# A hybrid decoder step: fewer transposes and products for the prompt's compressed branch and for a masked key block

## The chip, the cores and the metric

The kernel runs on one core of a Trainium2 chip. The core has TensorE (PE in the profile, with its weight loads as PEld), VectorE (DVE), ScalarE (ACT), GpSimd (POOL) and SyncE (SP), which work side by side and wait for each other through semaphores; 16 DMA engines move data. The metric is the device time of one execution in microseconds, as the median of several runs.

## What is computed

One layer of a decoder trunk is run on a prompt of 512 tokens and on 8 samples of 4 tokens. One input projection feeds two groups of eight heads: native sparse attention (three branches: compressed blocks, selected blocks, sliding window) and forgetting attention. The outputs are gated, multiplied by one output projection, and normed. What matters here is cut from the reference:

```python
def nsa_block(q, q_pos, gates, kc, vc, c_end, ks, vs, kw, vw, w_pos, slopes):
    ...
    p_c = masked_softmax(s_c, dist_c >= 0)
    o_c = jnp.einsum('bhgtn,bnhd->bthgd', p_c.astype(vc.dtype), vc)
    ...
    o = g[..., 0:1] * o_c + g[..., 1:2] * o_s + g[..., 2:3] * o_w

def fox_block(q, q_pos, dq, k, v, dk, k_pos):
    ...
    p = masked_softmax(s, k_pos[None, :] <= q_pos[:, None])
    return jnp.einsum('bhts,bshd->bthd', p.astype(v.dtype), v)
```

The prompt has 512 / 32 = 16 compressed keys, so `p_c` of a block of 128 queries is 128 x 16 for each head. In `fox_block` a query block sees no key block behind it.

## The kernel before

**Precision.** [...] `mm3` (L394) issues three products: hi x hi, hi x lo and lo x hi.

**What fills the time.** `run_tiles` (L515) computes the input projection: 60 tiles of 128 columns, each with 4 pieces of weights (`raw`, loaded from `w_in`, split into `whi` and `wlo`), into the PSUM tile `pz`, 272 tokens at a time. Its products are called pz products below. A piece is used by 24 of them, 12 for each half of the tokens; its split is issued two pieces ahead of use, and its load four splits ahead. `run_outputs` (L589) computes the output projection at the end, into `po`.

**What sets the order.** All other work (compression, both groups of heads on prompt and samples) is written as Python generators, the side streams. After every three pz products, `pump` (L223) lets each stream that is ready go on to its next `yield`. What is ready is decided by a clock that the recording layer keeps with its own costs for every instruction (class `Clock`); nothing of it is left at run time. The result is one fixed order for each engine. So a stream that issues less, or waits elsewhere, moves everything recorded after it. Every instruction goes through one helper line (L169), which is why the profile shows that line alone; groups are told apart by the names of their tiles.

**Forgetting attention on the prompt** (`fox_prompt`, L897). For each of 8 heads and each of two pairs of query blocks (`pr`), scores go to `fp` (probabilities, one tile for each of the two query blocks, `il`). The stream `apply` (L906) turns them: for each pair of key blocks (`jc`), four transposes of 128 x 128 into one PSUM tile `tr` (L923 to L927), then the split into `fpth` and `fptl` (128 x 512 each), then products with the split values `fvh`, `fvl` into `accf`. In the last pair of key blocks, the second one is masked for the first query block; those columns are filled with zeros (L987) and turned like the rest.

**Sparse attention on the prompt** (`nsa_prompt`, L1360). For each of two K/V heads, two pairs of query heads and four query blocks (16 jobs), the probabilities of the selected and the window branch are in tiles `np`, those of the compressed branch in `npc` (128 x 2 x 17; the last column is padding). The stream `apply` (L1378) turns `np` block by block, splits it into `npth` and `nptl` and multiplies by the values `nv0`, `nv1` into `acc`. At last it turns `npc`, one transpose of 128 x 16 for each of the two heads (L1413), splits the 16 x 256 result into `nptch` and `nptcl`, and adds three products with the compressed values `vcph`, `vcpl` (L1429). These tiles have 128 rows, of which 16 are filled and 112 hold zeros. `vcz` (L1386) is the load of the 16 rows of values.

**Samples.** `nsa_sample` (L1534) follows `nsa_prompt`; after it a tile `mx` is made, and `mix` (L1828) multiplies each head's output by its gate path, from loads. The output projection needs these heads one after another.

## Time and profile before

| what | us |
|---|---|
| median of 3 runs | 1379.68 |
| lowest, highest | 1375.85, 1386.52 |
| profiled execution, its own time | 1380.05 |
| span of the profiled execution | 1378.4 |

The page of the profile gives the busy time of each engine, the granted clock of TensorE in 40 slices (9 is 90% or more), and a chain of waits followed back from the last instruction. The view by windows gives busy times by stretch of the span, in us from its start; the timeline gives single instructions. The touched jobs run from 470 us (first transposes of `npc`) to 859 us (last), and from 518 us to 1073 us (first transposes of `fp` to last products into `accf`); the output products start at 1170 us.

### The profile page before, as it was taken

Reading aid. Unit: us, or ns where it says so; the run is one execution under the profiler, and the core shown is the slowest. Engines: PE = TensorE matmul, PEld = TensorE weight load, DVE = VectorE, ACT = ScalarE, POOL = GpSimd, SP = SyncE. Lnnn points to the kernel's source line nnn. Section 1 sums busy time; section 2 is a strip of 40 time slices with the busy share of each in tenths; the row PEclk is TensorE's granted clock in tenths of the full one; section 3 lists DMA queues with packets and bytes.
Section 4 is the critical chain, followed back from the end, with each engine's and each line's share of the span. In section 5 each row is a group of like instructions: output and inputs, shape, how many; then the busy total and the mean of one; then the engine's idle time right before and its main releaser. Section 6 shows DMA issues by size and latency. Waiting matters only on the chain.

```text
span 1378.4 us, 27307 instructions
## 1 busy us (share of the span) xinstructions
PE 1309.4 (95%) x10149; PEld 1151.8 (84%) x10149; DVE 789.9 (57%) x1982; ACT 544.6 (40%) x1167; POOL 276.2 (20%) x357
## 2 busy tenths in 40 slices
PE   8999898889999999998999999999999999999997
PEld 6899777778879999997888888788788899777786
DVE  6737655667644576655457774366466445444346
ACT  5224222323333467751224454136655423333222
POOL 3402435453430000004243302211110200000000
PEclk8999999999999999999999999999999999999999
DMA  6566667676998454467765758998788695234423
GB/s 193 170 168 192 204 176 224 206 231 196 282 298 243 116 145 150 147 180 219 254 201 178 217 151 247 249 255 218 222 207 187 209 321 162 72 121 147 129 90 130
DMA packets 303664, 265.65 MB, mean 193 GB/s; under 512 B 83058, under 2 KB 250850, under 8 KB 302860
## 3 DMA queue, kind: packets, MB, share of 16 engines
q1 hardware_dynamic: 279372, 187.30, 47.8%
q0 software_dynamic: 24016, 76.10, 17.4%
q8 instruction: 79, 1.29, 0.4%
q10 hardware_dynamic: 144, 0.52, 0.1%
q14 instruction: 53, 0.43, 0.1%
HBM read 235.68 MB, written 36.49 MB: 197 GB/s over the span
## 4 chain that ended last, share of the span: by engine, by line
PE 85%; DMA 5%; DVE 3%; issue 3%; ACT 1%; another core or an unknown queue 1%; SPq 1%; DVEq 0%; ACTq 0%
PE pz L169 48%; PE po L169 14%; PE s L169 6%; PE accv L169 5%; PE tr L169 5%; PE acc L169 3%; PE psb L169 2%; PE accf L169 1%; SPq L169 1%; DMA spg<-in_state_nsa_win 1%; DMA xt<-in_x_prompt 1%; DMA fpg<-in_cache_fox_kv 1%; DMA raw<-in_w_in 1%; PE pre L169 1%
## 5 line engine op out<-in xcount | busy, mean ns | idle before, releaser
L169 PE MATMUL pz<-h_hi,whi 128*128 128x272 f32 x1920 | 568.1, 296 | 11.2 <-ACT zt L169 4.7
L169 PE MATMUL pz<-h_hi,wlo 128*128 128x272 f32 x1920 | 557.6, 290 | 4.3 <-issue 3.5
L169 PE MATMUL pz<-h_lo,whi 128*128 128x272 f32 x1920 | 557.3, 290 | 3.7 <-issue 3.7
L169 PEld LDWEIGHTS pz<-h_hi,whi 128*128 128x128 f32 x1920 | 366.2, 191 | 30.1 <-issue 19.6
L169 PEld LDWEIGHTS pz<-h_lo,whi 128*128 128x128 f32 x1920 | 365.8, 191 | 5.4 <-issue 4.8
L169 PEld LDWEIGHTS pz<-h_hi,wlo 128*128 128x128 f32 x1920 | 365.3, 190 | 4.9 <-issue 3.8
L169 ACT ACTIVATE whi<-raw 128x512 fp32r<-128x512 f32 x275 | 171.6, 626 | 276.0 <-PE pz L169 142.8
L169 DVE TENSOR_TENSOR wlo<-raw,whi 128x512 fp32r<-128x512 f32 x275 | 185.9, 676 | 143.9 <-ACT whi L169 131.8
L169 POOL DMA_INDIRECT fpg<-in_cache_fox_kv,fi x128 | 127.6, 997 | 352.3 <-DMA raw<-in_w_in 205.9
L169 DVE TENSOR_TENSOR zt<-pz,rsb 128x272 f32<-128x272 f32 x61 | 26.9, 441 | 131.9 <-PE pz L169 128.1
L169 PE MATMUL po<-whi,h_hi 128*128 128x512 f32 (+1 forms) x256 | 95.5, 373 | 0.0
L169 PE MATMUL po<-whi,h_lo 128*128 128x512 f32 (+1 forms) x256 | 93.4, 365 | 0.0
L169 PE MATMUL po<-wlo,h_hi 128*128 128x512 f32 (+1 forms) x256 | 93.4, 365 | 0.0
L169 POOL DMA_INDIRECT crow<-in_cache_nsa_kv,ci x64 | 64.4, 1007 | 123.1 <-DVE ct L169 85.9
L169 ACT ACTIVATE zt<-pz 128x272 f32<-128x272 f32 x60 | 23.8, 396 | 155.0 <-PE pz L169 110.2
L169 DVE STREAM_TRANSPOSE ft<-fpg 128x1024 f32<-128x1024 f32 x64 | 78.6, 1232 | 8.9 <-PE accv L169 2.9
L169 POOL DMA_DIRECT2D spg<-in_cache_nsa_kv x64 | 35.0, 547 | 183.7 <-DVE skt L169 60.2
L169 PE MATMUL accv<-ft,fqb 128*32 128x256 f32 x512 | 51.0, 402 | 21.1 <-issue 19.8
L169 ACT ACTIVATE cxh<-ct 128x580 fp32r<-128x580 f32 (+1 forms) x64 | 42.2, 659 | 70.7 <-DVE ct L169 46.6
L169 DVE TENSOR_TENSOR cxl<-ct,cxh 128x580 fp32r<-128x580 f32 (+1 forms) x64 | 45.9, 717 | 39.2 <-ACT cxh L169 35.4
L169 PEld LDWEIGHTS po<-whi,h_hi 128*128 128x128 f32 x256 | 48.1, 188 | 19.7 <-ACT whi L169 7.5
L169 POOL DMA_DIRECT2D fpg<-in_cache_fox_kv x64 | 34.9, 545 | 135.6 <-PE accv L169 65.7
(412 smaller groups left out, 1965.8 us busy)
## 6 DMA issues: line engine op xcount, KB each, us to landing
raw<-in_w_in SPq DMA_DIRECT2D x240, 256.0 KB
fpg<-in_cache_fox_kv POOLq DMA_DIRECT2D x64, 256.0 KB
fpg<-in_cache_fox_kv SPq DMA_DIRECT2D x64, 256.0 KB
raw<-in_w_out SPq DMA_DIRECT2D x40, 256.0 KB
spg<-in_cache_nsa_kv POOLq DMA_DIRECT2D x64, 128.0 KB
spg<-in_cache_nsa_kv SPq DMA_DIRECT2D x64, 128.0 KB
out<-in_state_nsa_win SPq DMA_DIRECT2D x32, 254.0 KB
scr_z<-zt SPq DMA_DIRECT2D x28, 272.0 KB
```

The costliest lines, as they stand in the source:

```text
L169: return fn(*a, **k)
```

## The change

Three things are written otherwise.

*Forgetting attention.* In the last pair of key blocks the transpose of the masked block is left out. The two key blocks change places in the PSUM tile (`1 - jl`), so that the three turned blocks lie side by side; 384 columns are split instead of 512, and the first 128 columns of `fpth` and `fptl` are set to zero by VectorE. The memset of the masked columns of `fp` goes.

*Compressed probabilities.* The split is made before the transpose. A new tile `npx` (two of them, used in turn) holds for each of two heads 64 columns: the 16 rounded probabilities, the 16 remainders, the 16 rounded ones again, and 16 zeros. ScalarE writes the rounded ones (twice, by one instruction), VectorE the remainders. One transpose turns all 128 columns. From the 128 x 128 result ScalarE copies the upper 64 rows to the first 128 columns of `nptc`, and VectorE the lower 64 rows to the last 128 columns; the rest of `nptc` stays zero.

*Compressed values.* `vcp` holds, for each of two heads, the rounded values, the rounded values again, and the remainders, in rows that answer to those of `npx`. One product over 128 rows then gives hi x hi + lo x hi + hi x lo for both heads. `vcz` is loaded by two DMAs, each with the 16 rows three times, after a memset.

```diff
@@ fox_prompt, apply
-                                for il in range(2):
-                                    nc.tensor.transpose(tp[:, jl, il, :], pp[il][:, j * P:(j + 1) * P], ident)
+                                for il in range(jl if jc == pr else 0, 2):
+                                    nc.tensor.transpose(tp[:, 1 - jl, il, :], pp[il][:, j * P:(j + 1) * P], ident)
...
-                            yield from split((nxt[0], nxt[1], tp.rearrange("p j i t -> p j (i t)")))
+                            z = P if jc == pr else 0
+                            for x in nxt if z else ():
+                                nc.vector.memset(x[:, 0, :z].bitcast(F32), 0.0)
+                            yield from split(tuple(x.rearrange(y)[:, z:] for x, y in (
+                                (nxt[0], "p j t -> p (j t)"), (nxt[1], "p j t -> p (j t)"), (tp, "p j i t -> p (j i t)"))))
...
-                                mm3(acc, (v[0][:, js], v[1][:, js]), (last[0][:, jl, :], last[1][:, jl, :]),
+                                mm3(acc, (v[0][:, js], v[1][:, js]), (last[0][:, 1 - jl, :], last[1][:, 1 - jl, :]),
@@ fox_prompt
-                    if il == 0:
-                        nc.vector.memset(p[:, n:n + P], 0.0)
@@ nsa_prompt
+        pcx = [pl.tile([P, 2, 64], F32R, name=f"npx{x}") for x in range(2)]
+        for x in pcx:
+            nc.vector.memset(x[:, :, 48:].bitcast(F32), 0.0)
@@ nsa_prompt, apply
-                vc = pair(pl, [P, P], "vcp")
-                ptc = pair(pl, [P, 256], "nptc")
-                for x in (*vc, *ptc):
-                    nc.vector.memset(x.bitcast(F32), 0.0)
-                vcz = load(pl.tile([16, P], F32, name="vcz"), vp_scr[:, kvh, :])
+                vc = pl.tile([P, P], F32R, name="vcp")
+                ptc = pl.tile([P, 256], F32R, name="nptc")
+                vcz = pl.tile([P, P], F32, name="vcz")
+                nc.vector.memset(ptc.bitcast(F32), 0.0)
+                nc.vector.memset(vcz, 0.0)
+                for g in range(2):
+                    load(vcz[g * 64:g * 64 + 48], dram(vp_scr, kvh * P, [[0, 3], [2 * P, 16], [1, P]]))
...
-                yield from split((vc[0][:16], vc[1][:16], vcz))
+                cp(vc, vcz)
+                yield [vc]
+                for g in range(2):
+                    r = slice(g * 64 + 32, g * 64 + 64)
+                    low(vc[r], vc[r], vcz[r])
...
-                            tp = tr_tile([16, 2, P])
-                            for g in range(2):
-                                nc.tensor.transpose(tp[:, g, :], pc[:, g, :16], ident)
+                            tp = tr_tile([P, P])
+                            nc.tensor.transpose(tp, pc.rearrange("p g n -> p (g n)").bitcast(F32), ident)
...
-                            nxt = ptc
-                            yield from split((nxt[0][:16], nxt[1][:16], tp.rearrange("p g t -> p (g t)")))
+                            cp(ptc[:64, :P], tp[:64])
+                            nc.vector.tensor_copy(ptc[64:, P:], tp[64:])
+                            nxt = (ptc, ptc)
...
-                                mm3(acc, (vc[0], vc[1]), last, False, True)
+                                mm(acc, vc, ptc, False, True)
@@ nsa_prompt
-                    yield [sm]
+                    px = pcx[i % 2]
+                    yield [pc]
+                    cp(px.rearrange("p g (a n) -> p g a n", n=32)[:, :, :, :16], pc[:, :, None, :16].to_broadcast([P, 2, 2, 16]))
...
+                            nc.vector.tensor_tensor(px[:, :, 16:32], pc[:, :, :16], px[:, :, :16], op=OP.subtract)
-                    jobs.append((h0, i, pg, pc))
+                    jobs.append((h0, i, pg, px))
```

Where it moves instructions is seen at three places. A row is an instruction with its output, its inputs and its shape; a number after x counts equal rows. On PE, at the third job of the compressed branch before:

```order
L169 MATMUL acc<-npth,nv1l 128x256
L169 MATMUL pz<-h_hi,whi 128x272
L169 MATMUL pz<-h_lo,whi 128x272
L169 MATMUL pz<-h_hi,wlo 128x272
L169 MATMUL acc<-nptch,vcph 128x256
L169 MATMUL acc<-nptcl,vcph 128x256
L169 MATMUL acc<-nptch,vcpl 128x256
```

The same place on PE after:

```order
L169 MATMUL acc<-npth,nv1l 128x256
L169 MATMUL pz<-h_hi,whi 128x272
L169 MATMUL pz<-h_lo,whi 128x272
L169 MATMUL pz<-h_hi,wlo 128x272
L169 MATMUL acc<-nptc,vcp 128x256
L169 MATMUL tr<-nkh,nqh 128x16
```

Three products became one, behind the same three pz products. On PE, the first transposes of the forgetting branch before (two query blocks, two key blocks; 6143 and 6169 are the tiles of the two query blocks):

```order
L169 MATMUL pz<-h_hi,wlo 128x272
L169 MATMUL tr<-ident,fp_6143 128x128
L169 MATMUL tr<-ident,fp_6169 128x128
L169 MATMUL tr<-ident,fp_6143 128x128
L169 MATMUL tr<-ident,fp_6169 128x128
L169 MATMUL pz<-h_hi,whi 128x272
```

The same place on PE after (the two tiles are 6106 and 6156 here):

```order
L169 MATMUL pz<-h_hi,wlo 128x272
L169 MATMUL tr<-ident,fp_6106 128x128
L169 MATMUL tr<-ident,fp_6156 128x128 x2
L169 MATMUL pz<-h_hi,whi 128x272
L169 MATMUL pz<-h_lo,whi 128x272
```

The second transpose of the first query block is gone. On SP, the queue of loads where `vcz` of the first K/V head is loaded, before, with what each waits for (DVE is VectorE, DMAHW an earlier load):

```order
L169 DMA kcz<-scr_kp 128x32
L169 DMA nz<-scr_z 128x512 [waits DMAHW4_49]
L169 DMA vcz<-scr_vp 16x128 [waits DMAHW5_49]
L169 DMA nz<-out 128x4x128
L169 DMA out<-nat 4x32x32 [waits DVE_49]
```

The same place on SP after:

```order
L169 DMA kcz<-scr_kp 128x32
L169 DMA nz<-scr_z 128x512 [waits DMAHW4_49]
L169 DMA vcz<-scr_vp 48x1x128 [waits DMAHW5_49,DVE_49]
L169 DMA vcz<-scr_vp 48x1x128
L169 DMA nz<-out 128x4x128
```

The load of `vcz` now waits for VectorE, and what follows it in the queue stands behind that wait. Over the whole program, PE has 16 products less of each of two kinds (`nptch`, `nptcl` with their partners, 48 to 16), 16 transposes of `npc` less and 16 of `fp` less. All streams after the first jobs of `nsa_prompt` stand at other places among the pz products: the last products of `nsa_sample` come before 333 pz products that are left, where 444 were left.

## The prediction

> **What bounds the kernel now.** I read the page first: the busy line, the granted clock, the chain of waits.

> ```profile
> span 1378.4 us, 27307 instructions
> PE 1309.4 (95%) x10149; PEld 1151.8 (84%) x10149; DVE 789.9 (57%) x1982; ACT 544.6 (40%) x1167; POOL 276.2 (20%) x357
> ...
> PEclk8999999999999999999999999999999999999999
> ...
> PE 85%; DMA 5%; DVE 3%; issue 3%; ACT 1%; another core or an unknown queue 1%; SPq 1%; DVEq 0%; ACTq 0%
> ```

> TensorE (PE) is busy for 95% of the span and carries 85% of the chain; VectorE (DVE) and ScalarE (ACT) have 40% and more to spare. So an instruction taken off PE should be worth its own slot. Whether that holds where the change lies is read from the view by windows; each row is a stretch, its length, then busy us of PE, PEld, DVE, ACT and POOL, the granted clock, the DMA share and GB/s.

> ```profile
> 437.00:600.00 163.00, 162.56 (x1283) 157.86 (x1282) 108.86 (x376) 104.61 (x261) 0.00 (x0) 1.00 0.52 148
> 600.00:680.00 80.00, 72.09 (x537) 66.58 (x536) 39.13 (x86) 23.56 (x51) 20.13 (x20) 0.94 0.70 218
> 680.00:870.00 190.00, 183.29 (x1524) 159.34 (x1524) 116.47 (x327) 79.41 (x198) 56.24 (x68) 1.00 0.70 206
> 870.00:1075.00 205.00, 196.23 (x1714) 170.72 (x1709) 125.65 (x364) 105.23 (x207) 35.08 (x64) 0.98 0.86 221
> 1075.00:1170.00 95.00, 95.00 (x836) 87.68 (x835) 40.85 (x93) 28.45 (x50) 4.29 (x8) 1.00 0.71 233
> ```

> The touched branches run from 437 to 1075 us. In the first stretch PE idles 0.44 us of 163; in the next three 7.91, 6.71 and 8.77 us. The sum over the part that the change can reorder is 23.8 us, which is also the most that a better order could win there.

> A PE instruction's duration is not its price, since matmuls overlap. The price is the step from one start to the next. Three places in the timeline show it (start, duration, instruction):

> ```profile
> 470.85 0.38 PE L169 MATMUL tr<-ident,npc 128*16 128x128 f32 x2
> ...
> 471.20 0.29 PE L169 MATMUL pz<-h_lo,whi 128*128 128x272 f32 x1
> 471.32 0.29 PE L169 MATMUL pz<-h_hi,wlo 128*128 128x272 f32 x1
> ```

> ```profile
> 475.55 0.28 PE L169 MATMUL acc<-nptch,vcph 128*128 128x256 f32 x1
> ...
> 475.90 0.29 PE L169 MATMUL pz<-h_hi,whi 128*128 128x272 f32 x1
> ```

> ```profile
> 518.53 0.60 PE L169 MATMUL tr<-ident,fp 128*128 128x128 f32 x4
> 518.88 0.37 PE L169 MATMUL pz<-h_hi,whi 128*128 128x272 f32 x1
> 519.09 0.29 PE L169 MATMUL pz<-h_lo,whi 128*128 128x272 f32 x1
> ```

> A pz product steps by about 0.12 us (471.20 to 471.32). The pair of compressed transposes takes 471.20 - 470.85 = 0.35 us with one pz product (0.125) in it: 0.11 us each. The three compressed products take 475.90 - 475.55 = 0.35 us: 0.117 each. Four full transposes take 519.09 - 518.53 = 0.56 us with one pz product: 0.109 each. A transpose from 16 columns costs PE as much as one from 128.

> **The change part by part.** The counts are in the groups by shape (count, busy us, mean ns, idle before):

> ```profile
> L169 PE MATMUL tr<-ident,fp 128*128 128x128 f32 x96 | 14.7, 274 | 0.2 <-ACT fp L169 0.2
> ...
> L169 PE MATMUL tr<-ident,npc 128*16 128x128 f32 x32 | 6.1, 272 | 0.0
> ...
> L169 PE MATMUL acc<-nptcl,vcph 128*128 128x256 f32 x16 | 4.6, 287 | 1.0 <-DVE nptcl L169 1.0
> ```

> Compressed transposes: 32 become 16, so 16 x 0.11 = 1.8 us less on PE. Compressed products: 48 become 16, so 32 x 0.117 = 3.7 us less. The product that stays is of the same shape, with 112 of its rows in use instead of 16. Forgetting branch: of the 96 transposes, the one whose key block is masked goes in each of 8 heads x 2 pairs: 16 x 0.109 = 1.7 us. Sum on PE: 1.8 + 3.7 + 1.7 = 7.2 us.

> [...]

> What the other engines get, by their nearest rows:

> ```profile
> L169 DVE TENSOR_TENSOR nptcl<-tr,nptch 16x256 fp32r<-16x256 f32 x16 | 6.4, 403 | 3.8 <-ACT nptch L169 3.8
> L169 DVE TENSOR_TENSOR npc<-npr,nst 128x34 f32<-128x34 f32 x16 | 3.1, 195 | 0.5
> L169 DVE MEMSET fp<- 128x128 f32 x16 | 2.6, 165 | 0.0
> L169 DVE COPY fpt<-tr 128x128 f32<-128x128 f32 x8 | 2.1, 282 | 1.6 <-ACT fpt L169 1.6
> ```

> ```profile
> L169 ACT ACTIVATE fpth<-tr 128x512 fp32r<-128x512 f32 x24 | 14.2, 593 | 17.3 <-PE tr L169 17.2
> L169 ACT ACTIVATE nptch<-tr 16x256 fp32r<-16x256 f32 x16 | 5.8, 365 | 15.4 <-PE tr L169 11.6 <-remote 3.7
> L169 ACT ACTIVATE npc<-npc 128x34 f32<-128x34 f32 x16 | 3.6, 225 | 6.4 <-DVE npc L169 6.4
> L169 ACT ACTIVATE fpt<-tr 128x128 f32<-128x128 f32 x8 | 2.1, 278 | 6.9 <-DVE fpt L169 3.9 <-DVE fpn L169 3.0
> ```

> DVE, compressed branch, per job: the 403 ns subtraction behind the transpose goes, a copy of 128 columns (282) and a subtraction of 32 (195) come: +74 ns, x16 = +1.2 us. ACT, per job: 365 goes, a copy of 128 columns (278) and one of 64 (between 225 and 278, say 245) come: +158 ns, x16 = +2.5 us. Forgetting branch: two memsets of 165 ns for one, and 384 columns split instead of 512. Estimated by the ratio of columns, the split saves at most a quarter of its 593 ns on ACT, and something like that on DVE: together about zero. The cover for these 4 us is the idle third of both engines in the busiest stretch (DVE 109 and ACT 105 of 163 us). If it is gone, they cost at most the 3.7 us of additions. I take nothing.

> The wait between transpose and product. Before, ScalarE rounds, then VectorE subtracts, then PE goes on. After, ScalarE copies one half and VectorE's copy of the other half still stands behind it, by the written order of the tile. Two engines in a row remain, 278 + 282 ns instead of 365 + 403. In 16 jobs PE sat idle for this 1.0 us in all (the nptcl row above), so the gain lies between 0 and 1 us. A loss is possible if VectorE comes to the copy later than to the subtraction; the same row bounds that to about a microsecond. I take zero.

> The wait on the load queue (SP). The load of vcz now waits for VectorE's memset, and the weight loads stand behind it in that queue. The two rows of the queue and of VectorE:

> ```profile
> 437.75 3.92 SPq L169 DMA_DIRECT2D out<-nat  x5
> 441.78 0.45 SPq L169 DMA_DIRECT2D raw<-in_w_in  x1
> ```

> ```profile
> 439.51 0.27 DVE L169 MEMSET nptcl<- 128x256 f32 x1
> ```

> The queue went on at 437.75; now it may start about 439.8, 2 us later. A weight piece is loaded four splits ahead, and a piece serves 24 pz products, 24 x 0.125 = 3 us, so 12 us are in hand: nothing on the path. The upper bound is the 2 us, once; for the second K/V head the load was behind the memsets already.

> Moved work. The recording layer places side work between pz products by its own clock, so all of it after 437 us moves. The sum of work is the same; what differs is which waits PE meets. The nearest rows are two bad stretches of 20 us, with their idle PE and low clock:

> ```profile
> 640.00:660.00 20.00, 14.93 (x99) 11.95 (x102) 9.58 (x15) 2.81 (x5) 8.03 (x9) 0.84 0.86 282
> ...
> 1000.00:1020.00 20.00, 17.22 (x119) 15.58 (x118) 11.21 (x52) 8.17 (x19) 3.30 (x6) 0.83 1.09 256
> ```

> The first costs 5.1 us of idle and 0.16 x 20 = 3.2 us of clock, 8.3 us in all; the second 2.8 + 3.4 = 6.2 us. One such stretch more or less is what the new order can do: -8 to +8 us. I take zero in between, as nothing shows a side.

> Sum: -7.2 us. The profiled execution took 1380.05 us (its span of 1378.4 and 1.65 around it), 0.4 us over the median of 1379.68, so 1380.05 - 7.2 = 1373 us.

> **The rivals.** *Gain taken back as waiting:* the branch is on PE's path where PE is full, but PE then meets the sample heads' page loads earlier. For it: DMA share 0.86 over 870 to 1075 us and 1.09 at 1000. Against it: the pages are fetched as buffers come free, which moves with PE. It would give back all 7 us: 1380.

> *More than the sum:* a shorter compressed chain and freed transposition buffers let the order close a bad stretch as well: 1373 - 8 = 1365. For it: 23.8 us of idle PE there. Against it: nearly all of that idle time stands at page loads and sample products, which the change does not touch.

> *Slower:* the sample stage of native sparse attention ends later in the order, with 333 pz products left instead of 444, which is 111 x 0.125 = 14 us nearer to the output products. Its end starts the mixing of 16 heads, from loads:

> ```profile
> 1114.31 0.36 DVE L169 COPY o_s<-tr 128x64 f32<-128x64 f32 x2 [5.75 <-PE tr L169]
> 1122.18 0.68 DVE L169 TENSOR_TENSOR mx<-mx,oz 128x512 f32<-128x512 f32 x1
> ...
> 1150.15 0.18 DVE L169 TENSOR_TENSOR o_s<-mx,o_s 128x32 f32<-128x32 f32 x1
> ```

> ```profile
> 1169.89 199.06 PE po L169 x1152
> ```

> Fourteen heads are mixed within 1150 - 1114 = 36 us, and 1170 - 1114 = 56 us are there. So a shift of up to 20 us is free, and every microsecond past it is added to the end. The order alone gives 14. From a shift of 27 us on (20 and the 7 gained) the kernel is slower than before, from 40 us on by over 1%: 1373 + 20 = 1393. For it: the DMA engines are at 0.71 to 0.86 of their time there, and PE would meet the last heads' loads together with the weights. Against it: the output products take the heads one after another, so the late ones have more room than I count.

> [...]

> *The change doesn't do what it says:* the order shows 16 compressed products and 80 forgetting transposes, so PE's count is certain; only the time is open.

> **How the numbers follow.** The sum arrives, 1367 to 1379: 0.58. Taken back, about 1380: 0.22. More than the sum, 1365 or less: 0.12. Slower, 1380 to 1393 and beyond: 0.08. About 1% is what a measurement of this kernel can tell from no change: the runs shown reach from 1375.85 to 1386.52. 1% of 1379.68 is 13.8 us, so faster means under 1365.9 and slower over 1393.5. Faster 0.12; slower by over 1% is the worse half of that rival, 0.04; same 0.84. The range takes in the bad stretch on either side of the sum and the spread of runs of a few us: 1363 to 1383.

> **What would show it.** In the profile after: 16 products of acc with nptc and none with nptch; 16 transposes of npx; 80 of fp; PE busy some 7 us less and the stretch from 437 us to the last accf product shorter by 5 us or more; clock and idle after 870 us as before. Wrong would be: PE idle between 437 and 1170 us well over 24 us, a granted clock under 0.9 in slices where it was 1.00, or PE waiting for mx before its first output products.

## The result and the profile after

| | median us | lowest to highest | runs |
|---|---|---|---|
| before, same series | 1381.76 | 1375.85 to 1391.03 | 10 |
| after | 1372.25 | 1367.97 to 1379.73 | 10 |

The ratio is 0.9937, with a 95% interval of 0.9915 to 0.9959. By this ratio it is 8.7 us less (5.7 to 11.7; the medians differ by 9.5), where 7.2 were forecast. The profiled execution of after is the slowest of its ten (1379.73 us), so its span must not be held against the span before. Up to the 2275th pz product TensorE has the same instructions in the same order in both, and the after profile reaches it at 456.7 us, before at 451.0. From there to the last pz product, the stretch in which the change lies, it took 712.1 us against 718.5, 6.4 less. From the last pz product to the end of the span it is 208.8 us in after and 208.5 in before.

The page of after: busy times, granted clock and chain.

```profile
span 1378.1 us, 27228 instructions
PE 1306.8 (95%) x10085; PEld 1153.1 (84%) x10085; DVE 792.7 (58%) x2014; ACT 546.9 (40%) x1185; POOL 276.9 (20%) x357
...
PEclk9999989888999999999999999999999999999999
...
PE 77%; issue 8%; DMA 6%; DVE 3%; POOL 2%; SPq 1%; ACT 1%; another core or an unknown queue 1%; POOLq 0%; DVEq 0%; ACTq 0%
```

PE has 64 instructions less (10149 to 10085) and 2.6 us less busy time in this execution, because the part ahead of the change was slower in it: up to the 2275th pz product PE was busy for 418.6 us, before for 415.3, with the same instructions. The slices with an 8 in the clock lie between 172 and 345 us, ahead of the touched code. The windows of before, taken again on after:

```profile
437.00:600.00 163.00, 163.00 (x1286) 158.01 (x1279) 111.83 (x397) 105.20 (x269) 0.00 (x0) 1.00 0.53 151
600.00:680.00 80.00, 71.34 (x544) 67.36 (x544) 38.44 (x89) 23.42 (x50) 19.32 (x20) 0.94 0.73 225
680.00:870.00 190.00, 184.09 (x1530) 162.50 (x1528) 121.83 (x340) 81.84 (x207) 59.25 (x70) 0.98 0.71 209
870.00:1075.00 205.00, 196.60 (x1694) 171.22 (x1693) 119.48 (x363) 102.84 (x202) 30.81 (x56) 0.98 0.84 217
1075.00:1170.00 95.00, 94.66 (x822) 86.13 (x821) 45.24 (x98) 32.30 (x58) 7.54 (x14) 1.00 0.75 244
```

PE idles 0 + 8.66 + 5.91 + 8.40 + 0.34 = 23.3 us, as against 23.8 before. In the sum of idle time nothing was lost and nothing gained. The slots themselves are in PE's timeline, at the first compressed job:

```profile
476.56 0.27 PE L169 MATMUL tr<-ident,npx 128*128 128x128 f32 x1
476.58 0.37 PE L169 MATMUL pz<-h_hi,whi 128*128 128x272 f32 x1
476.80 0.29 PE L169 MATMUL pz<-h_lo,whi 128*128 128x272 f32 x1
...
479.25 0.28 PE L169 MATMUL acc<-nptc,vcp 128*128 128x256 f32 x1
479.37 0.29 PE L169 MATMUL pz<-h_hi,whi 128*128 128x272 f32 x1
```

From the transpose to the second pz product are 0.24 us, which is 0.115 for the transpose beside a pz product's 0.125. The one product that is left steps by 0.12 us. Both are the prices of the forecast, and to the 0.01 us of the timeline a product with 96 filled rows costs no more here (0.12 us) than one with 16 did before (0.117).

The groups by shape (busy us and mean ns, then the idle time before them):

```profile
L169 PE MATMUL tr<-ident,fp 128*128 128x128 f32 x80 | 13.0, 275 | 0.3 <-ACT fp L169 0.3
...
L169 ACT ACTIVATE fpth<-tr 128x384 fp32r<-128x384 f32 x16 | 7.8, 485 | 13.1 <-PE tr L169 13.1
...
L169 PE MATMUL tr<-ident,npx 128*128 128x128 f32 x16 | 4.4, 275 | 0.0
L169 ACT ACTIVATE npx<-npc 128x64 fp32r<-128x64 f32 x16 | 4.0, 250 | 6.9 <-DVE npc L169 5.5 <-DVE nsc L169 1.3
...
L169 DVE CAST nptc<-tr 64x128 fp32r<-64x128 f32 x16 | 4.7, 294 | 10.8 <-ACT nptc L169 10.6
L169 PE MATMUL acc<-nptc,vcp 128*128 128x256 f32 x16 | 4.7, 291 | 0.0
L169 ACT ACTIVATE nptc<-tr 64x128 fp32r<-64x128 f32 x16 | 4.3, 267 | 15.5 <-PE tr L169 15.4
```

PE never waits for `nptc` (0.0 us), where it had waited 1.0 us for `nptcl`. VectorE's copy of the lower half does wait for ScalarE's copy of the upper half (10.6 us), as they are still one behind the other.

### The profile page after: what moved, and what is told of

It reads as the page before. It is cut to its first block, busy times and chain, and to the rows that moved or that the text cites. A ratio compares the mean times of both kernels' runs of the same rounds, so it can differ in the third digit from the quotient of the medians.

```text
span 1378.1 us, 27228 instructions
## 1 busy us (share of the span) xinstructions
PE 1306.8 (95%) x10085; PEld 1153.1 (84%) x10085; DVE 792.7 (58%) x2014; ACT 546.9 (40%) x1185; POOL 276.9 (20%) x357
## 3 DMA queue, kind: packets, MB, share of 16 engines
q0 software_dynamic: 24016, 76.10, 17.5%
## 4 chain that ended last, share of the span: by engine, by line
PE 77%; issue 8%; DMA 6%; DVE 3%; POOL 2%; SPq 1%; ACT 1%; another core or an unknown queue 1%; POOLq 0%; DVEq 0%; ACTq 0%
PE pz L169 43%; PE po L169 14%; PE accv L169 5%; PE s L169 5%; PE tr L169 4%; PE acc L169 3%; DMA fpg<-in_cache_fox_kv 2%; POOL fpg L169 2%; PE psb L169 1%; PE accf L169 1%; DMA raw<-in_w_in 1%; SPq L169 1%; DMA xt<-in_x_prompt 1%; DMA spg<-in_cache_nsa_kv 1%
## 5 line engine op out<-in xcount | busy, mean ns | idle before, releaser
L169 PE MATMUL pz<-h_hi,whi 128*128 128x272 f32 x1920 | 571.3, 298 | 14.1 <-ACT whi L169 6.4
L169 PE MATMUL pz<-h_hi,wlo 128*128 128x272 f32 x1920 | 560.6, 292 | 5.6 <-issue 2.8
L169 PE MATMUL pz<-h_lo,whi 128*128 128x272 f32 x1920 | 560.2, 292 | 4.9 <-issue 4.8
L169 PEld LDWEIGHTS pz<-h_hi,whi 128*128 128x128 f32 x1920 | 369.0, 192 | 33.4 <-issue 18.5
L169 PEld LDWEIGHTS pz<-h_hi,wlo 128*128 128x128 f32 x1920 | 368.0, 192 | 8.6 <-issue 4.5
L169 PEld LDWEIGHTS pz<-h_lo,whi 128*128 128x128 f32 x1920 | 368.9, 192 | 5.7 <-issue 4.9
L169 ACT ACTIVATE whi<-raw 128x512 fp32r<-128x512 f32 x275 | 171.6, 626 | 280.6 <-PE pz L169 120.9
L169 DVE TENSOR_TENSOR wlo<-raw,whi 128x512 fp32r<-128x512 f32 x275 | 186.1, 678 | 164.1 <-ACT whi L169 151.6
L169 POOL DMA_INDIRECT fpg<-in_cache_fox_kv,fi x128 | 127.9, 999 | 346.2 <-DMA out<-nat 203.1
L169 DVE TENSOR_TENSOR zt<-pz,rsb 128x272 f32<-128x272 f32 x61 | 26.9, 440 | 119.6 <-PE pz L169 98.4
L169 PE MATMUL po<-whi,h_hi 128*128 128x512 f32 (+1 forms) x256 | 95.5, 373 | 0.0
L169 PE MATMUL po<-whi,h_lo 128*128 128x512 f32 (+1 forms) x256 | 93.4, 365 | 0.0
L169 PE MATMUL po<-wlo,h_hi 128*128 128x512 f32 (+1 forms) x256 | 93.4, 365 | 0.0
L169 POOL DMA_INDIRECT crow<-in_cache_nsa_kv,ci x64 | 64.5, 1008 | 130.1 <-DVE ct L169 91.2
L169 DVE STREAM_TRANSPOSE ft<-fpg 128x1024 f32<-128x1024 f32 x64 | 79.0, 1235 | 10.0 <-PE accv L169 3.9
L169 ACT ACTIVATE zt<-pz 128x272 f32<-128x272 f32 x60 | 23.9, 398 | 151.8 <-PE pz L169 102.7
L169 POOL DMA_DIRECT2D spg<-in_cache_nsa_kv x64 | 35.1, 548 | 192.0 <-DVE skt L169 113.4
L169 DVE TENSOR_TENSOR cxl<-ct,cxh 128x580 fp32r<-128x580 f32 (+1 forms) x64 | 46.0, 718 | 35.1 <-ACT cxh L169 29.2
L169 ACT ACTIVATE cxh<-ct 128x580 fp32r<-128x580 f32 (+1 forms) x64 | 42.1, 658 | 60.1 <-DVE ct L169 45.1
L169 PEld LDWEIGHTS po<-whi,h_hi 128*128 128x128 f32 x256 | 48.1, 188 | 19.7 <-ACT whi L169 7.5
L169 PE MATMUL accv<-ft,fqb 128*32 128x256 f32 x512 | 46.9, 415 | 17.1 <-issue 16.5
L169 POOL DMA_DIRECT2D fpg<-in_cache_fox_kv x64 | 35.2, 549 | 138.1 <-PE accv L169 97.1
```

Of the source, the lines that this page charges most:

```text
L169: return fn(*a, **k)
```

## The experiments

The forecast stands on two claims: each instruction taken off PE is worth its slot, and the order that the planner makes of the rest is worth nothing on the average. The theory was that both hold, so that a kernel's time is its slots plus the luck of its order. The first rival was that the slots vanish in slack and the order makes the gain, the second that one of the two parts has a cost of its own on the other engines. Ratios are to the kernel before in the same series of runs, since that kernel's median was not the same in all of them: 1376.17 us in the series of the first four runs, 1303.97 in that of the next three, 1381.57 in that of the four after these, and 1304.32 in that of the last.

**Each part alone.** The compressed branch alone (the lines of the forgetting branch put back):

```diff
-                                for il in range(jl if jc == pr else 0, 2):
-                                    nc.tensor.transpose(tp[:, 1 - jl, il, :], pp[il][:, j * P:(j + 1) * P], ident)
+                                for il in range(2):
+                                    nc.tensor.transpose(tp[:, jl, il, :], pp[il][:, j * P:(j + 1) * P], ident)
...
```

> Only the compressed branch is changed; the masked key block is turned as before. If the gain is the sum of PE's slots, 16 transposes and 32 products fewer give 16 x 0.11 + 32 x 0.117 = 5.5 us, a ratio of about 0.996. If it is the luck of one order, this third order lands anywhere within some 5 us of before, on either side. If the masked block brings most of it, the ratio is 0.999 or more.

Measured: 1359.6 us, ratio 0.9884 (0.9858 to 0.9911). That is 16.0 us less for slots of 5.5, more than the whole change saves. And the masked block alone, the same edit the other way round on the kernel before:

> Only the masked key block is left unturned; the compressed branch is as before. By PE's slots: 16 x 0.109 = 1.7 us, a ratio of 0.9988, which an interval of 0.2% will hardly tell from 1. By the luck of the order: anywhere within some 5 us of before.

Measured: 1383.68 us, ratio 1.0068 (1.0040 to 1.0096): 9.4 us more, though PE has 16 instructions less. Neither agrees with its slots, and the two differ from them in opposite directions, by 10.5 and 11.1 us. So a new order is worth more than was allowed, or the masked block costs something that the forecast doesn't have.

**Slots in a fixed order.** To price the slots without the order, instructions were added or left out behind the planner's back. First, 12 more products with a tile of zeros (`none`) in each compressed job of the changed kernel, all else in its place:

```diff
+                                for _ in range(12):
+                                    nc.nc.tensor.matmul(acc, vc, none[:, None, :].to_broadcast([P, 4, 64]), start=False, stop=False, skip_group_check=True)
                                 mm(acc, vc, ptc, False, True)
```

> The changed kernel in its own order, with twelve products of 256 zero columns added to each of the 16 compressed products; the recording layer does not count them, so every other instruction stays in its place. If PE's slots are the price, 192 x 0.117 = 22.5 us come on top: a ratio to before of 0.9937 + 0.0163 = 1.010. If PE has slack at these places, and the gain came from the order, the ratio stays near 0.994.

Measured: 1381.88 us, ratio 1.0058 (1.0036 to 1.0080). Against the 0.9937 of after, measured in another series, this is 0.0121, some 16.7 us for 192 products whose slots are 22.5 (in the run with the old slots, below, two such products take 0.23 us, from 476.18 to 476.41 us). Then the kernel before, with two of its three compressed products planned but not issued:

```diff
-                                mm3(acc, (vc[0], vc[1]), last, False, True)
+                                mm(acc, vc[0], last[0], False, True)
+                                for x, y in ((vc[0], last[1]), (vc[1], last[0])):
+                                    clock.note("pe", "matmul", (acc, x, y), {})
```

> The kernel before in its own order, with two of the three compressed products counted by the recording layer but not issued (the compressed branch loses its low parts). By PE's slots: 32 x 0.117 = 3.7 us less, a ratio of 0.9973, and up to 1 us more for the wait on nptcl that goes with them. By the order: 1.000, since the order is that of before.

Measured: 1371.39 us, ratio 0.9967 (0.9943 to 0.9991), 4.5 us less (1.2 to 7.8) for slots of 3.7 and the wait for `nptcl` of up to 1.0 that goes with them. In a fixed order the slots arrive, as far as this interval tells.

**The order alone.** One constant of the planner (what it allows for a semaphore between engines, 0.25) was set to 0.26. No instruction changes, only the order.

```diff
-    HOP = 0.25
+    HOP = 0.26
```

> The kernel before with one number of the recording layer's clock changed (the hop between engines, 0.25 to 0.26), so that the same instructions come in another order from the compression on. If orders hardly differ in time, 1.000 within 0.2%. If the luck of an order is worth as much as the change, it lies 0.3% or more off, on either side.

> The changed kernel with the same number changed. By PE's slots it keeps about 7 us against the shaken kernel before, whatever that one gives: a ratio to before of 0.994 if orders do not matter. By the luck of the order: anywhere from 0.990 to 1.002.

Measured: before with this order 1307.39 us, ratio 1.0031 (1.0015 to 1.0047); after with it 1310.27 us, 1.0039 (1.0022 to 1.0056). The kernel before loses 4 us by its order alone. Shaken after stands 0.0008 above shaken before, and its slots should have put it 0.0055 below: here the order took the whole gain. A third run kept after's instructions and gave the planner the old kernel's PE costs:

```diff
                                 mm(acc, vc, ptc, False, True)
+                                clock.t["pe"] += 0.34
```

(and 0.11 for each masked pair.)

> The changed kernel, with the recording layer's clock moved on by 0.34 us at each compressed product and 0.11 us at each masked block, as if PE still did the removed work. Same instructions, an order nearer to that of before. By PE's slots: 0.9945 as for the change, within 0.3%. If the change lives from its own order: 0.998 or more.

Measured: 1308.45 us, ratio 1.0029 (1.0009 to 1.0048). Old costs did not bring back an order as good as the old one. After in its own order was not run in this series, so what of these two ratios belongs to this series, in which the kernel before is quicker too, stays open.

**Both in one series.** After and the compressed branch alone were run again, the latter also with the shaken order, and with them the run that parts the change in two: after in its own order, with the 64 lost PE instructions put back unplanned.

```diff
+                                    for _ in range(1 if jc == pr and jl else 0):
+                                        nc.nc.tensor.transpose(tp[:, 1 - jl, il, :], pp[il][:, j * P:(j + 1) * P], ident)
                                     nc.tensor.transpose(tp[:, 1 - jl, il, :], pp[il][:, j * P:(j + 1) * P], ident)
...
+                            nc.nc.tensor.transpose(tp, pc.rearrange("p g n -> p (g n)").bitcast(F32), ident)
                             nc.tensor.transpose(tp, pc.rearrange("p g n -> p (g n)").bitcast(F32), ident)
...
+                                for _ in range(2):
+                                    nc.nc.tensor.matmul(acc, vc, none[:, None, :].to_broadcast([P, 4, 64]), start=False, stop=False, skip_group_check=True)
                                 mm(acc, vc, ptc, False, True)
```

> The changed kernel once more, so that it stands beside the next three in the same series. Both theories expect the ratio that it had, 0.9937 (0.9915 to 0.9959). Should the series be one with a quicker input projection, as the last one was, with less idle time to win or lose in the order, the slots of 7.2 us alone would give 1 - 7.2/1307 = 0.9945.

> The compressed branch alone once more, as in the first experiment. Theory 'slots, and the luck of the order': its gain beyond the slots (5.5 us, ratio 0.996) is an order that meets fewer waits, so it is the same program with the same order and gives 0.988 again where the chip serves the loads as it did then; where it serves them quicker, there is less to win and the ratio lies between 0.988 and 0.996. Rival 'the masked block costs something of its own on the engines': 0.988 again under both, and after at 0.994 above it.

> The compressed branch alone, its order shaken by one constant of the planner (0.25 to 0.26), which changes no instruction. Theory 'slots, and the luck of the order': the extra gain of 0.008 goes with the order, and the ratio comes back towards the slots alone, 0.996, with some 0.004 on either side for the luck of the new order; at least 0.003 above the run with the unshaken order. Rival 'the masked block costs something of its own': the order has nothing to do with it, and the ratio stays within 0.002 of the unshaken run.

> The changed kernel in its own order, instruction by instruction, with the 64 TensorE instructions that the change took away put back without the planner seeing them: two products with a zero operand in each of the 16 compressed jobs, a second issue of each compressed transpose, and one transpose more in each of the 16 masked pairs. If the change's slots are on the path, it is 7.2 us, or 0.0052 to 0.0055 of the time, slower than the changed kernel in the same series. What is left against the kernel before is the new order (and the work moved to the other engines) alone: prediction's zero says 1.000, and the surplus of the first measurement, 8.7 - 7.2 = 1.5 us, says 0.999. If the slots were in slack and the order made the gain, it is the same as the changed kernel within 0.002.

| run | median us | ratio to before | 95% |
|---|---|---|---|
| after again | 1372.81 | 0.9949 | 0.9926 to 0.9971 |
| compressed branch alone, again | 1365.67 | 0.9903 | 0.9870 to 0.9937 |
| the same, shaken order | 1375.04 | 0.9963 | 0.9942 to 0.9983 |
| after, old slots put back | 1377.93 | 0.9976 | 0.9950 to 1.0003 |

Three things follow. Putting the slots back costs 5.1 us by the medians and 4.0 by the means (resampling the twelve runs of each gives 1.0 to 7.0 for the means), in an order that is the same row for row: most of the gain is the slots, a little less than the 7.2 of the forecast. What is left, the order and the moved work, is 0.9976, 3.3 us to the good and no more than the interval. And the compressed branch alone gives its surplus again (13.4 us for slots of 5.5) but loses it with the order: shaken it is 9.4 us slower (5.2 to 13.2 for the means), and stands at the 0.996 of its slots. That surplus was luck of the order.

In the profiles the order's part is a matter of waits that come back at the same place. PE's timeline around two of after's waits, in after, in its repetition and in the run with the old slots, both of a later series; the bracket is the idle time and what ended it:

```profile
762.08 1.11 PE L169 MATMUL tr<-ident,np 128*128 128x128 f32 x4 [2.89 <-DVE nptl L169]
...
932.12 0.59 PE L169 MATMUL pz<-h_hi,whi 128*128 128x272 f32 x1 [2.08 <-ACT whi L169]
```

```profile
758.43 1.12 PE L169 MATMUL tr<-ident,np 128*128 128x128 f32 x4 [2.88 <-DVE nptl L169]
...
928.58 0.60 PE L169 MATMUL pz<-h_hi,whi 128*128 128x272 f32 x1 [3.28 <-ACT whi L169]
```

```profile
759.92 1.11 PE L169 MATMUL tr<-ident,np 128*128 128x128 f32 x4 [2.46 <-DVE nptl L169]
...
929.71 0.40 PE L169 MATMUL pz<-h_hi,whi 128*128 128x272 f32 x1 [3.58 <-ACT whi L169]
```

The compressed branch alone never has the second. The first it has too, at the same transpose (the 97th of `np` in PE's order), but shorter: 0.71 us in the repetition, 1.53 in the first measurement.

```profile
755.72 0.66 PE L169 MATMUL tr<-ident,np 128*128 128x128 f32 x4 [0.71 <-DVE nptl L169]
```

Its windows, in the repetition, from 600 us on:

```profile
600.00:680.00 80.00, 75.47 (x634) 71.94 (x634) 46.76 (x98) 27.78 (x60) 23.59 (x24) 1.00 0.81 252
680.00:870.00 190.00, 184.85 (x1527) 161.47 (x1526) 117.07 (x332) 81.66 (x209) 57.29 (x73) 1.00 0.73 214
870.00:1075.00 205.00, 200.02 (x1792) 174.03 (x1795) 130.02 (x379) 112.26 (x215) 31.54 (x58) 1.00 0.83 217
```

The clock is 1.00 throughout, and PE idles 4.5 + 5.2 + 5.0 us, against 8.7 + 5.9 + 8.4 in after at a clock of 0.94 to 0.98. That profile is the fastest of its six executions, after's the slowest of its ten, so the difference is larger than that of the medians. With the other order, the same branch met two waits:

```profile
873.45 0.36 PE L169 MATMUL pz<-h_hi,whi 128*128 128x272 f32 x1 [2.85 <-DVE zt L169]
878.33 0.59 PE L169 MATMUL pz<-h_hi,whi 128*128 128x272 f32 x1 [3.00 <-ACT zt L169]
```

Behind the second stands ScalarE's queue. Its part of the split of the weights (it copies `raw` into `whi`, and VectorE subtracts that for `wlo`) came after 12.24 us of idling that their load ended; `zt` was behind it:

```profile
877.37 0.63 ACT L169 ACTIVATE whi<-raw 128x512 fp32r<-128x512 f32 x1 [12.24 <-DMA raw<-in_w_in]
877.90 0.38 ACT L169 ACTIVATE zt<-pz 128x272 f32<-128x272 f32 x1
```

**The masked block with another order.** If the masked block's loss is luck of the order too, another order should take it away.

> The masked block alone, its order shaken by the same constant (0.25 to 0.26). Unshaken it came out at 1.0068, though its 16 slots of 1.7 us alone give 0.9988. Theory 'slots, and the luck of the order': the loss belonged to that order and goes with it, back to 0.9988 with some 0.004 on either side, at least 0.003 below 1.0068. Rival 'the masked block costs something of its own' (its memsets stand in front of the split on VectorE, and PE waits for the split): the ratio stays within 0.002 of 1.0068 in any order.

Measured: 1320.63 us, ratio 1.0122 (1.0099 to 1.0146). It did not go; it grew. The theory fails here in its plain form. Nor is the rival's mechanism in the trace: PE waits 0.4 us in all in front of the 80 transposes of `fp`, and 0.0 in front of the products into `accf`. What both kernels with the masked block alone share, and the kernel before has not, is a wait of PE for the sample branch's keys. Shaken after, which has the masked block too, has it as well (5.1 us in two waits), but after in its own order has not, so the block does not bring it in every order; the compressed branch alone has at most 1.2 us of it. The waits of PE, by what they wait for (us in all, times, longest), first in the unshaken kernel, then in the shaken:

```profile
PE s L169 <- DMA kvc<-scr_kc: 5.8, 2, 3.1
PE pz L169 <- ACT zt L169: 4.6, 2, 3.9
```

```profile
PE s L169 <- DMA kvc<-scr_kc: 5.9, 2, 3.7
```

And what such a wait costs beyond itself, in the timeline of the shaken kernel:

```profile
832.26 0.29 PE L169 MATMUL pz<-h_lo,whi 128*128 128x272 f32 x1
832.39 0.29 PE L169 MATMUL pz<-h_hi,wlo 128*128 128x272 f32 x1
836.41 1.31 PE L169 MATMUL s<-kvc,qv 128*128 128x256 f32 x4 [3.74 <-DMA kvc<-scr_kc]
...
837.98 0.43 PE L169 MATMUL pz<-h_hi,wlo 128*128 128x272 f32 x1
838.20 0.43 PE L169 MATMUL pz<-h_hi,whi 128*128 128x272 f32 x1
...
840.68 0.30 PE L169 MATMUL pz<-h_hi,wlo 128*128 128x272 f32 x1
840.81 0.29 PE L169 MATMUL pz<-h_hi,whi 128*128 128x272 f32 x1
```

Behind 3.74 us of idling the pz products step by 0.22 to 0.23 us instead of 0.125, until 840.7: the twelve steps from 837.98 to 840.68 take 2.70 us, 1.2 us more than at 0.125. The other wait of the unshaken kernel shows how a load gets there. ScalarE's queue held a split of forgetting attention's values whose load was issued at 931.73 us, 6.7 us earlier, and the `zt` that PE needed stood behind it:

```profile
938.40 0.63 ACT L169 ACTIVATE fvh<-fvz 128x512 fp32r<-128x512 f32 x1 [8.92 <-DMA fvz<-out]
...
939.98 0.37 ACT L169 ACTIVATE zt<-pz 128x272 f32<-128x272 f32 x1
```

None of these waits is at an instruction that the masked block adds. But all four comparisons with and without it have it on the slow side: alone against before (0.0068); alone against before, both shaken (1.0122 against 1.0031, two series); after against the compressed branch (0.9949 against 0.9903, one series); the same, both shaken (1.0039 against 0.9963, two series). Four of four may still be chance, once in eight if either side is as likely. Whether the masked block's edit leads the planner to worse orders for a reason, or four draws fell alike, is not settled.

The times of the stretch, from the 2275th pz product to the last, for the profiled executions; the idle time of PE and the time lost to a lower clock while it was busy are summed from its records and the granted clock's, and the last column is what is left, its work at full clock:

| kernel | total us | idle | lost to the clock | rest |
|---|---|---|---|---|
| before | 718.5 | 23.8 | 7.1 | 687.6 |
| after | 712.1 | 23.3 | 11.9 | 676.9 |
| after again | 708.1 | 20.6 | 9.8 | 677.7 |
| after, old slots put back | 714.1 | 20.8 | 10.0 | 683.3 |
| compressed branch alone | 698.4 | 15.3 | 4.5 | 678.6 |
| the same again | 694.1 | 14.7 | 0.0 | 679.5 |
| the same, shaken | 717.7 | 22.6 | 12.2 | 683.0 |
| masked block alone | 732.0 | 30.3 | 15.8 | 685.9 |

The rest goes down by 5.6 us from the old slots to the new in one order (683.3 to 677.7). It is no pure count of slots: with equal instructions it spreads by 4.4 us (678.6 to 683.0). Between before and after with the old slots, which issue equally many PE instructions, it differs by 4.3 us, so it also holds something of the order. A wait that only uses up the part of a product's shown time by which products overlap (0.29 us shown, 0.125 us of step) does not count as idle; how much of the 4.3 us that is was not followed.

Idle and lost clock together reach from 14.7 to 46.1 us. Before has 30.9 and after 30.4 to 35.2: in these two the change exchanged one middling order for another. Each row is one execution. Those of after, of the shaken run and of the masked block are the slowest of their series and that of the compressed branch again is the fastest, so the rows lie further apart than the medians do (717.7 and 694.1 us for medians that differ by 9.4).

## Why the prediction was right

*The sum of 7.2 us.* Right in kind and nearly in size. The order shows the 64 instructions gone, the timeline shows their price (steps of 0.11 to 0.12 us for a transpose of 128 columns, 0.12 for a product), and in a fixed order they are worth 4.0 to 5.1 us (1.0 to 7.0), with 4.5 for 3.7 forecast in the old order. The 192 added products gave 16.7 of 22.5. So a slot is worth three quarters to all of its step, and a part of it lies where PE would have waited anyway. The profile with the added products shows this: reckoned as in the table, its rest is 697.7 us, 20.0 to 20.8 more than after's, while its idle time (17.5) and lost clock (7.5) are 5.4 to 10.2 us less together.

*The other engines.* ScalarE got 2.3 us (546.9 - 544.6) where 2.5 were forecast. VectorE got 2.8 (792.7 - 789.9) for 1.2; the forgetting branch's zero is about 0.5 us of that, since two memsets (330 ns) and a subtraction of 384 columns (551) stand for one memset (165) and a subtraction of 512 (685); the rest was not followed. All hidden, as assumed: no wait of PE names a tile that the added work writes.

*The wait between transpose and product.* Taken as zero within 0 to 1 us of gain: it is the upper end, 1.0 us to 0.0. The two copies do stand one behind the other.

*The wait on the load queue.* Right that it is hidden, wrong in size. SP's queue stood from 441.57 to 445.20, 3.6 us and not 2, until VectorE's memset at 445.0:

```profile
441.14 0.43 SPq L169 DMA_DIRECT2D nz<-scr_z  x1
445.20 1.59 SPq L169 DMA_DIRECT2D vcz<-scr_vp  x2
```

```profile
445.00 0.17 DVE L169 MEMSET vcz<- 128x128 f32 x1
```

The window from 437 to 600 us has PE busy for 163.00 of 163 us, so none of it came through.

*The moved work.* Taken as zero between -8 and +8 us. Zero was right for this order (0.9976, so -3.3 us, interval -6.9 to +0.4). The bounds were wrong. "One bad stretch more or less" was too small: orders of equal or nearly equal work stand, beyond their slots, from 10.5 us to the good (the compressed branch alone) to 11.1 to the bad (the masked block alone), and 17.6 in the series at 1304 us (15.9 measured and 1.7 of slots). The forecast of the whole was right because the order that was drawn is a middling one, by luck, which nothing in the profile of before could show. The range of 20 us held, with luck too; the sizes found here ask for one of about 30.

*The rivals.* "Gain taken back as waiting" did not happen in this order and did in the shaken one. "More than the sum" was argued against because the idle time stands at loads and sample products that the change does not touch. That reasoning failed: the compressed branch alone touches them no more, and its order took idle time and lost clock from 30.9 to between 14.7 and 19.8 us. A wait need not be touched to be moved. The ceiling of 23.8 us for what a better order could win was too low as well: it counts the idle time and leaves out the 7.1 us that the same stretch loses to the clock. "Slower", by a late sample stage: its last products moved as the order said, and PE did not wait for `mx`. The group before, then after, with its first and last start:

```profile
L169 PE MATMUL acc<-spg,PT x192: 379/379/636, 979.3 to 1112.4; 128*32 128x256 f32 x192
```

```profile
L169 PE MATMUL acc<-spg,PT x192: 379/379/404, 996.8 to 1125.6; 128*32 128x256 f32 x192
```

13.2 us later for 14 forecast, inside the 20 that were said to be free.

*What would show it.* The counts, the idle sum (23.3 us for "well over 24") and the mean clock after 870 us are as named. One sign of being wrong did appear in the windows of 20 us that the prediction used: from 760 to 780 us the granted clock was 1.00 before and is 0.83 after, while the bad stretch from 1000 to 1020 us is gone (0.83 before, 1.00 after). First before, then after:

```profile
760.00:780.00 20.00, 17.82 (x152) 15.68 (x151) 14.34 (x36) 10.22 (x24) 8.89 (x10) 1.00 0.69 207
```

```profile
760.00:780.00 20.00, 17.62 (x130) 15.98 (x131) 14.76 (x41) 9.77 (x24) 7.76 (x8) 0.83 0.48 144
```

So the order changed in its parts, and only the sum stayed. PE's busy time is not as named: 2.6 us less for 7, because it contains the first 457 us, where the same instructions were busy for 3.3 us more. The prediction also counts 112 rows in use in the product that stays; they are 96 (2 heads x 3 x 16), which changes no term. The stretch between two fixed instructions was the right measure (6.4 us), and the busy line was not.

## What to carry to other kernels

In a kernel bound by one engine whose instruction order is planned ahead, price an edit by its slots, and give the new order a term of its own with bounds taken from measured reorderings: here up to 11 us either way in the ordinary series, as much as the edit or more. To know what an edit is worth, put its instructions back without moving anything; to know what an order is worth, shake it by a constant that changes nothing else. When one part alone beats the whole, as the compressed branch did twice (0.9884 and 0.9903, against 0.9937 and 0.9949), it may be only the better draw: it is the faster kernel as it stands, and its surplus goes with the next edit.

## What the hardware showed besides

In the stretch that can be reordered PE idles seven times for 2 us or more in these two traces; in six of them the clock is at 0.5 in the gap or within 1.5 us of its end. The seventh is 2.33 us long, ends at 886.0 us in before, and falls into two windows, neither of which was idle for more than 1.82 us; a gap of 2.08 us in after, which ends at 932.12, has the clock at 0.5 from 931.94 on. So in these two traces the length of a wait alone does not tell its cost; how it falls on the grid does.

The same kernel took 1376 to 1382 us in three series and 1304 in two. The difference shows long before the touched code. From 160 to 240 us, in the compressed branch alone (first measurement) and in after with the old costs, of the series at 1304 us; up to 470 us both have the same instructions in the same order on every engine, and both ran on the same chip:

```profile
160.00:240.00 80.00, 67.22 (x519) 58.87 (x518) 48.73 (x74) 19.65 (x44) 43.60 (x44) 0.94 0.74 215
```

```profile
160.00:240.00 80.00, 80.00 (x717) 74.64 (x717) 66.96 (x105) 29.80 (x66) 58.54 (x58) 1.00 0.97 297
```

In the second, PE is full and the DMA engines move 297 GB/s instead of 215. One chip gave both, at different times, so it is not the chip. Between 100 and 440 us the first has 23.8 us of idle PE for which the profile names no releaser ("issue"), the second none. The cause is open.
